# Branch products in pairs, lambda on ScalarE, bias turning in four pieces and value products with their low parts last, in a two-layer hybrid encoder

## The chip, the cores and the metric

The kernel runs on one core of one Trainium2 chip. The metric is device time in microseconds (us) of one execution. The engines are named as in the profile: PE is TensorE (matmuls and transposes), DVE is VectorE, ACT is ScalarE, POOL is GpSimd and SP is SyncE, which here issues the weight loads.

## The reference, cut to what matters

Two layers, each an FFN, a mixer and a second FFN, on 512 tokens of width 1024, all in fp32. The change touches the mixer alone:

```
qa, ka, va, qd, kd, vd, qc, kc, vc = jnp.split(h @ w_in[l], PROJ_OFFSETS, axis=-1)
ya = neighbourhood_attention(qa, ka, va, na_rpb[l])               # 8 heads, 2-D bias
# differential attention, 4 heads, two softmax maps each, T5 bias:
a = p[:, :, 0] - lam * p[:, :, 1]
yb = rms_norm(einsum(a, vd), subln_g) * (1.0 - lam_init)
yc = window_gqa(qc, kc, vc, gqa_sink[l], rel_bias_table)          # 8 query heads, 2 key heads
g = sigmoid(h @ w_gate[l] + b_gate[l])                            # 3 gates of width 1024
merged = g[0] * (ya @ w_branch[l, 0]) + g[1] * (yb @ w_branch[l, 1]) + g[2] * (yc @ w_branch[l, 2])
x = x + merged @ w_o[l]
```

## The kernel before

Activations stand turned, as 128 features by 512 tokens. Every fp32 operand of a product is split into a high and a low part, and a product is three matmuls for each 128 rows of the contraction: high weight by high input (L96), high weight by low input (L97) and, when all inputs have had these two, low weight by high input (L99). A weight tile is loaded by SP, its high part is cast on ACT (L82) and its low part is subtracted on DVE (L83). An input is split in the same way, by ACT L106 and DVE L108.

PSUM holds three buffers for products (`mm`), two for scores (`s`), two that transposes (`t`) and small statistics (`st`) share, and one for attention outputs and, once a layer, a fourth value block (`av`). A product takes a `mm` buffer, and gives it back when its reader is done: DVE L450 for a projection, DVE L797 for a gate, DVE L812 for a branch product.

The mixer writes its work down in an order made by hand. `beside(attention, steps, n)` takes eight attention steps, each with the transposes and value products left over from earlier steps, and puts some n of the listed projection, gate and merge steps between them. A scheduler then places the instructions of all of this on each engine, and may move them within it, so code that is written one product after another need not run so.

The places that the change and the prediction touch:

- `v_stacked` (L499 to L520) makes the values of the neighbourhood attention: four token blocks in four PSUM buffers (three `mm`, one `av`), all four filled in step over eight pieces of the contraction, then read by ACT L517 and DVE L518 in halves.
- `attend_diff` turns the head's bias on POOL (L675, one copy a head of 128x896), and after each pair of softmax maps takes the reciprocals of their sums on DVE (L739), multiplies the second by minus lambda on DVE (L740, 128x1), scales the second map on ACT (L741), and adds the two on DVE (L742). The result is transposed on PE (L681).
- `gqa_keys` projects keys and then values; the values, scaled by DVE L450, are transposed on PE (L832).
- `merge(i, mm)` makes two output tiles of branch i, each a product over the four 128-row pieces `yp` of that branch's attention output. The fourth piece comes last. For branch 1 it is made by DVE L714, then split by ACT L106 and DVE L108. The four merges of branch 2 stand at the end of the mixer, ahead of the output projection, with the attention's last fold ahead of them (ACT L568, DVE L569).

Of the kernel before, what the change touches and what calls it, by code (L numbers as in the profile page):

```python
# [13 lines left out]
AF = mybir.ActivationFunctionType  # L14
ALU = mybir.AluOpType

P = 128
# [16 lines left out]
def encoder(ctx: ExitStack, tc: tile.TileContext, a: dict, out: bass.AP):  # L34
# [51 lines left out]
    def mm_tile():  # L86
        return psum.tile([P, S], F32, tag="mm", name="mm", bufs=3)
# [4 lines left out]
    def product(ps, wparts, xhi, xlo):  # L92

        n = len(wparts)
        for k, (wh, wl) in enumerate(wparts):
            nc.tensor.matmul(ps, wh, xhi[k], start=k == 0, stop=False)  # L96
            nc.tensor.matmul(ps, wh, xlo[k], start=False, stop=False)  # L97
        for k, (wh, wl) in enumerate(wparts):
            nc.tensor.matmul(ps, wl, xhi[k], start=False, stop=k == n - 1)  # L99
# [74 lines left out]
    def reversed_view(t, last, dims):  # L174

        return bass.AP(tensor=t.tensor, offset=t.offset + last, ap=[list(t.ap[0]), *[[-s, n] for s, n in dims]])
# [252 lines left out]
    def mixer(l, h, nxt):  # L429
        with tc.tile_pool(name="mix", bufs=1) as mp:  # L430
# [68 lines left out]
            def v_stacked():  # L499

                ps = [mm_tile(), mm_tile(), mm_tile(), av_tile()]
                for c in range(4):
                    w = cols(weights(a["w_va"][l, c]), 2, S)
                    for k, (wh, wl) in enumerate(w, 2 * c):
                        for t in range(4):
                            ts = slice(t * P, (t + 1) * P)
                            nc.tensor.matmul(ps[t], h.hi[k][:, ts], wh, start=k == 0, stop=False)
                            nc.tensor.matmul(ps[t], h.lo[k][:, ts], wh, start=False, stop=False)
                            nc.tensor.matmul(ps[t], h.hi[k][:, ts], wl, start=False, stop=k == KC - 1)
                    yield  # L510
                v_na.extend(([], []))
                for t in range(4):
                    r = h.rs[:, t : t + 1]
                    for half in range(2):
                        v = mp.tile([P, 4, P], F32R, tag="v", name="vn", bufs=8)
                        pv = ps[t][:, half * 256 : half * 256 + 256].rearrange("p (h d) -> p h d", d=64)
                        nc.scalar.activation(v[:, :, 0:64], pv, AF.Copy, scale=r)  # L517
                        nc.vector.scalar_tensor_tensor(  # L518
                            out=v[:, :, 64:P], in0=pv, scalar=r, in1=f(v[:, :, 0:64]), op0=ALU.mult, op1=ALU.subtract
                        )  # L520
                        v_na[half].append(v)
                yield
# [145 lines left out]
            def attend_diff(head):  # L668
# [3 lines left out]
                db = work.tile([P, 640], F32, tag="acc", name="db", bufs=1)  # L672
                nc.sync.dma_start(db[:, 0:560], at(d_diff, head * 1024, [[1, 16], [64, 8], [1, 560]]))
                bias = mp.tile([P, 112, ROWS], F32, tag="pb", name="dpb", bufs=2)
                nc.gpsimd.tensor_copy(out=bias, in_=reversed_view(db, 559, [[1, 112], [GRID, ROWS]]))  # L675
                held = []

                def turn(half, jj, p, ph, pl):
# [38 lines left out]
                for half in range(2):  # L717
                    ph = mp.tile([P, 4, 2, P], F32R, tag="pt", name="ph", bufs=4)
                    pl = mp.tile([P, 4, 2, P], F32R, tag="pt", name="pl", bufs=4)
                    for jj in range(2):  # L720
                        j = 2 * half + jj
                        negm = small.tile([P, 4], F32, tag="negm", name="negm")
                        tot = small.tile([P, 4], F32, tag="tot", name="tot")
                        pc = []
                        for c in range(2):
                            ps = s_tile()
                            scores(ps, q[c], k[c], slice(j * P, j * P + P), slice(0, S))
                            pc.append(l_tile())
                            softmax(
                                pc[c],  # L730
                                ps,
                                bias[:, 48 - 16 * j : 112 - 16 * j].rearrange("p c r -> p (c r)"),
                                BIG,
                                negm[:, c : c + 1],
                                tot[:, c : c + 1],
                            )
                            if c == 0:
                                yield None
                        nc.vector.reciprocal(tot[:, 0:2], tot[:, 0:2])  # L739
                        nc.vector.tensor_tensor(out=tot[:, 1:2], in0=tot[:, 1:2], in1=nlam, op=ALU.mult)  # L740
                        nc.scalar.activation(pc[1], pc[1], AF.Copy, scale=tot[:, 1:2])  # L741
                        nc.vector.scalar_tensor_tensor(  # L742
                            out=pc[0], in0=pc[0], scalar=tot[:, 0:1], in1=pc[1], op0=ALU.mult, op1=ALU.add
                        )
                        yield lambda half=half, jj=jj, p=pc[0], ph=ph, pl=pl: turn(half, jj, p, ph, pl)
# [57 lines left out]
            def merge(i, mm):  # L803
                yh, yl = [t[0] for t in ys[i]], [t[1] for t in ys[i]]
                w = cols(weights(a["w_branch"][l, i, mm]), 8)
                for odd in range(2):
                    m = 2 * mm + odd
                    ps = mm_tile()
                    product(ps, w[4 * odd : 4 * odd + 4], yh, yl)
                    t = gates.pop((i, m))  # L810
                    o = merged[m] if i == 0 else t
                    nc.vector.scalar_tensor_tensor(out=o, in0=t, scalar=1.0, in1=ps, op0=ALU.add, op1=ALU.mult)  # L812
                    if i > 0:
                        nc.vector.tensor_tensor(out=merged[m], in0=merged[m], in1=t, op=ALU.add)
                    if i == 2:
                        mh[m] = mp.tile([P, S], F32R, tag="qk", name="mh", bufs=12)
                        nc.scalar.copy(mh[m], merged[m])
                        ml[m] = mp.tile([P, S], F32R, tag="v", name="ml", bufs=8)
                        nc.vector.tensor_tensor(out=ml[m], in0=merged[m], in1=f(mh[m]), op=ALU.subtract)
                yield  # L820

            def gqa_keys():
# [4 lines left out]
                    kd.append((t, swapped(t)))  # L827
                yield
                vf = project(21, 1.0, True)
                vt = t_tile()  # L830
                for t in range(4):
                    nc.tensor.transpose(vt[:, t, :], vf[:, t * P : (t + 1) * P], ident)  # L832
# [60 lines left out]
            beside(attend_diff(0), [qk(5), (None,), (None,), merge(0, 0), *g0(3, 4), merge(0, 1)], 8)  # L893
            beside(attend_diff(1), [g0(5)[0], merge(0, 2), qk(6), v_diff(1)], 6)
            beside(attend_diff(2), [*g0(6, 7), qk(7)], 4)
            beside(attend_diff(3), [merge(0, 3), gqa_keys(), gqa_queries(0), *g1(0, 1)], 6)
            beside(attend_gqa(0), [*g1(2), *[gqa_queries(p) for p in (1, 2, 3)], merge(1, 0), *g1(3)], 6)
            beside(attend_gqa(1), [*g1(4), merge(1, 1), *g1(5, 6), merge(1, 2), *g1(7)], 6)
            beside(attend_gqa(2), [merge(1, 3), *[gate(2, m, "v", 8) for m in range(3)]], 4)
            beside(attend_gqa(3), [gate(2, 3, "v", 8), *[gate(2, m) for m in (4, 5)]], 3)  # L900
# [114 lines left out]
```

## Time and profile before

| what | value |
|---|---|
| median of 3 runs (lowest to highest) | 2483.62 us (2482.66 to 2483.65) |
| the profiled execution's own time | 2485.75 us |
| its span in the trace | 2484.0 us |
| PE busy | 2465.3 us, 99% of the span, 11604 matmuls and transposes |
| DVE busy | 1294.3 us, 52% |
| ACT busy | 1053.8 us, 42% |
| POOL busy | 193.1 us, 8% |
| the chain that ended last | PE 97%, DVE 1%, ACT 1% |
| granted TensorE clock, mean | 0.999 of full speed |

Busy times are those of the trace. A matmul of 512 columns is listed with some 0.39 us, but the next one starts some 0.23 us after it, since they are pipelined. So a gap between the starts of two matmuls that is longer than that is time lost, also where the trace lists no idle time.

### The profile page before, as it was taken

How to read it: one execution, taken by the hardware profiler on the slowest of the kernel's cores; microseconds unless marked ns; L12 is line 12 of the kernel's file. 1: busy time of each engine (PE TensorE's matmuls, PEld its weight loads, DVE VectorE, ACT ScalarE, POOL GpSimd, SP SyncE). 2: the span in 40 equal slices, each digit the busy share in tenths (PEclk: the TensorE clock that was granted, in tenths of full speed). 3: DMA queues.
4: the chain of work that ended last, by engine and by line, in shares of the span. 5: the costliest groups of instructions: out<-in, count | busy, mean ns of one | idle time of the engine just before them, and what ended most of it. 6: DMA issues, size and time to landing. Idle time of an engine off the chain costs nothing.

```text
span 2484.0 us, 30196 instructions
## 1 busy us (share of the span) xinstructions
PE 2465.3 (99%) x11604; PEld 2054.7 (83%) x11604; DVE 1294.3 (52%) x2178; ACT 1053.8 (42%) x1776; POOL 193.1 (8%) x300
## 2 busy tenths in 40 slices
PE   8999999999999999999999999999999999999998
PEld 7888888888888888888888888888888888888887
DVE  5444335766666644443344443367676766444432
ACT  5333225755557433332232332267555664333322
POOL 2000003311000000000000000033110001000000
PEclk9999999999999999999999999999999999999999
DMA  5323344432322342233432324443322224332232
GB/s 169 102 94 100 119 131 127 118 103 78 93 85 86 124 128 97 95 98 119 133 107 94 101 91 131 140 118 107 98 86 92 86 83 148 119 115 93 95 100 68
DMA packets 80655, 265.24 MB, mean 107 GB/s; under 512 B 10904, under 2 KB 16328, under 8 KB 80512
## 3 DMA queue, kind: packets, MB, share of 16 engines
q1 hardware_dynamic: 67680, 226.59, 29.4%
q0 software_dynamic: 11680, 34.86, 4.9%
q8 instruction: 92, 1.51, 0.2%
q10 hardware_dynamic: 1152, 1.86, 0.2%
q14 instruction: 51, 0.42, 0.1%
HBM read 241.22 MB, written 12.62 MB: 102 GB/s over the span
## 4 chain that ended last, share of the span: by engine, by line
PE 97%; DVE 1%; ACT 1%; issue 0%; DMA 0%; SPq 0%; POOLq 0%; POOL 0%; ACTq 0%; DVEq 0%
PE mm L96 22%; PE mm L97 22%; PE mm L99 22%; PE mm L288 5%; PE mm L290 5%; PE mm L287 5%; PE av L597 2%; PE t L587 1%; PE s L542 1%; PE s L543 1%; PE av L698 1%; PE mm L492 1%; PE mm L491 1%; PE mm L389 1%; PE mm L387 1%; PE mm L388 1%
## 5 line engine op out<-in xcount | busy, mean ns | idle before, releaser
L96 PE MATMUL mm<-h,whi 128*128 128x512 f32 x2112 | 831.7, 394 | 0.2
L97 PE MATMUL mm<-l,whi 128*128 128x512 f32 x2112 | 825.0, 391 | 0.0
L82 ACT CAST whi<-raw 128x1024 fp32r<-128x1024 f32 (+1 forms) x414 | 429.9, 1039 | 715.3 <-PE mm L97 372.7
L83 DVE TENSOR_TENSOR wlo<-raw,whi 128x1024 fp32r<-128x1024 f32 (+1 forms) x414 | 500.6, 1209 | 294.3 <-ACT whi L82 179.7
L99 PE MATMUL mm<-h,wlo 128*128 128x512 f32 x2112 | 521.8, 390 | 0.0
L99 PEld LDWEIGHTS mm<-h,wlo 128*128 128x128 f32 x2112 | 396.7, 188 | 82.2
L96 PEld LDWEIGHTS mm<-h,whi 128*128 128x128 f32 x2112 | 397.0, 188 | 80.7 <-issue 0.8
L97 PEld LDWEIGHTS mm<-l,whi 128*128 128x128 f32 x2112 | 397.3, 188 | 79.4
L298 DVE TENSOR_TENSOR un<-mm,rb 128x512 f32<-128x512 f32 x87 | 60.1, 691 | 296.8 <-PE mm L99 296.8
L288 PE MATMUL mm<-g,whi 128*128 128x512 f32 x528 | 205.7, 390 | 0.0
L287 PE MATMUL mm<-g,whi 128*128 128x512 f32 x528 | 205.6, 389 | 0.0
L106 ACT CAST g<-un 128x512 fp32r<-128x512 f32 x88 | 54.5, 620 | 251.4 <-DVE un L299 251.4
L290 PE MATMUL mm<-g,wlo 128*128 128x512 f32 x528 | 131.4, 390 | 0.0
L295 DVE TENSOR_TENSOR gn<-mm,rb 128x512 f32<-128x512 f32 x88 | 60.8, 691 | 133.4 <-PE mm L99 133.4
L556 ACT ACTIVATE lg<-lg,negm 128x256 f32<-128x256 f32 (+1 forms) x192 | 114.0, 594 | 25.2 <-DVE negm L553 23.7
L61 POOL DMA_DIRECT2D d_x<-x x40 | 22.1, 553 | 1262.9 <-DVE x L246 1262.6
L288 PEld LDWEIGHTS mm<-g,whi 128*128 128x128 f32 x528 | 99.2, 188 | 20.5
L290 PEld LDWEIGHTS mm<-g,wlo 128*128 128x128 f32 x528 | 99.2, 188 | 20.5
L287 PEld LDWEIGHTS mm<-g,whi 128*128 128x128 f32 x528 | 99.1, 188 | 20.5
L296 ACT ACTIVATE gn<-gn 128x512 f32<-128x512 f32 x88 | 55.8, 634 | 123.6 <-DVE gn L295 123.6
L108 DVE TENSOR_TENSOR g<-un,g 128x512 fp32r<-128x512 f32 x88 | 60.9, 692 | 62.8 <-ACT g L106 62.8
L246 DVE SCALAR_TENSOR_TENSOR x<-mm,x 128x512 f32<-128x512 f32 x40 | 27.7, 692 | 109.1 <-PE mm L290 72.4
(223 smaller groups left out, 3037.8 us busy)
## 6 DMA issues: line engine op xcount, KB each, us to landing
raw<-in_w_gu SPq DMA_DIRECT2D x172, 512.0 KB, 3.4
raw<-in_w_down SPq DMA_DIRECT2D x48, 512.0 KB, 3.5
raw<-in_w_gate SPq DMA_DIRECT2D x48, 512.0 KB, 3.5
raw<-in_w_qk SPq DMA_DIRECT2D x44, 512.0 KB, 3.6
raw<-in_w_branch SPq DMA_DIRECT2D x24, 512.0 KB, 3.5
raw<-in_w_last SPq DMA_DIRECT2D x22, 512.0 KB, 3.5
d_x<-x POOLq DMA_DIRECT2D x40, 256.0 KB, 2.4
x<-d_x POOLq DMA_DIRECT2D x40, 256.0 KB, 2.9
```

Source lines behind the costliest of these rows:

```text
L82: nc.scalar.copy(hi[:, w], raw[:, w])
L83: nc.vector.tensor_tensor(out=lo[:, w], in0=raw[:, w], in1=f(hi[:, w]), op=ALU.subtract)
L96: nc.tensor.matmul(ps, wh, xhi[k], start=k == 0, stop=False)
L97: nc.tensor.matmul(ps, wh, xlo[k], start=False, stop=False)
L99: nc.tensor.matmul(ps, wl, xhi[k], start=False, stop=k == n - 1)
L108: nc.vector.tensor_tensor(out=lo, in0=src, in1=f(hi), op=ALU.subtract)
L287: nc.tensor.matmul(ps, w[k][0], ghi[c + k], start=c + k == 0, stop=False)
L288: nc.tensor.matmul(ps, w[k][0], glo[c + k], start=False, stop=False)
L290: nc.tensor.matmul(ps, w[k][1], ghi[c + k], start=False, stop=c + k == MF - 1)
L295: nc.vector.tensor_tensor(out=gn, in0=pg, in1=h.rb, op=ALU.mult)
L298: nc.vector.tensor_tensor(out=un, in0=pu, in1=h.rb, op=ALU.mult)
L556: nc.scalar.activation(p, p, AF.Exp, bias=negm, scale=-1.0, accum_out=total)
```

## The change

Five edits, all in the mixer, which runs once in each of the two layers.

1. `v_stacked`: for the first three weight tiles the high matmuls of both contraction pieces run first and the low ones behind them. With the last weight tile the four token blocks are finished one by one, each with its reads by ACT and DVE right behind.
2. The bias of a differential head is turned in four copies of 128x224 in place of one of 128x896.
3. The multiplication by minus lambda (128x1) is a ScalarE activation in place of a VectorE operation.
4. `merge`: the two output tiles are made side by side. Input by input, both take their two high matmuls; the low matmuls of the first and then of the second tile end it.
5. `gqa_keys` has one more `yield`, between the projection of the values and their transposes; the step counts of two `beside` calls go from 6 to 7 and from 6 to 5.

```
@@ -499,17 +499,30 @@
             def v_stacked():
 
                 ps = [mm_tile(), mm_tile(), mm_tile(), av_tile()]
-                for c in range(4):
+                def high(t, k, wh):
+                    ts = slice(t * P, (t + 1) * P)
+                    nc.tensor.matmul(ps[t], h.hi[k][:, ts], wh, start=k == 0, stop=False)
+                    nc.tensor.matmul(ps[t], h.lo[k][:, ts], wh, start=False, stop=False)
+
+                def low(t, k, wl):
+                    nc.tensor.matmul(ps[t], h.hi[k][:, t * P : (t + 1) * P], wl, start=False, stop=k == KC - 1)
+
+                for c in range(3):
                     w = cols(weights(a["w_va"][l, c]), 2, S)
-                    for k, (wh, wl) in enumerate(w, 2 * c):
+                    for k, (wh, _) in enumerate(w, 2 * c):
                         for t in range(4):
-                            ts = slice(t * P, (t + 1) * P)
-                            nc.tensor.matmul(ps[t], h.hi[k][:, ts], wh, start=k == 0, stop=False)
-                            nc.tensor.matmul(ps[t], h.lo[k][:, ts], wh, start=False, stop=False)
-                            nc.tensor.matmul(ps[t], h.hi[k][:, ts], wl, start=False, stop=k == KC - 1)
+                            high(t, k, wh)
+                    for k, (_, wl) in enumerate(w, 2 * c):
+                        for t in range(4):
+                            low(t, k, wl)
                     yield
+                w = cols(weights(a["w_va"][l, 3]), 2, S)
                 v_na.extend(([], []))
                 for t in range(4):
+                    for k, (wh, _) in enumerate(w, 6):
+                        high(t, k, wh)
+                    for k, (_, wl) in enumerate(w, 6):
+                        low(t, k, wl)
                     r = h.rs[:, t : t + 1]
                     for half in range(2):
                         v = mp.tile([P, 4, P], F32R, tag="v", name="vn", bufs=8)
@@ -672,7 +685,8 @@
                 db = work.tile([P, 640], F32, tag="acc", name="db", bufs=1)
                 nc.sync.dma_start(db[:, 0:560], at(d_diff, head * 1024, [[1, 16], [64, 8], [1, 560]]))
                 bias = mp.tile([P, 112, ROWS], F32, tag="pb", name="dpb", bufs=2)
-                nc.gpsimd.tensor_copy(out=bias, in_=reversed_view(db, 559, [[1, 112], [GRID, ROWS]]))
+                for c in range(0, 112, 28):
+                    nc.gpsimd.tensor_copy(out=bias[:, c : c + 28], in_=reversed_view(db, 559 - c, [[1, 28], [GRID, ROWS]]))
                 held = []
 
                 def turn(half, jj, p, ph, pl):
@@ -737,7 +751,7 @@
                             if c == 0:
                                 yield None
                         nc.vector.reciprocal(tot[:, 0:2], tot[:, 0:2])
-                        nc.vector.tensor_tensor(out=tot[:, 1:2], in0=tot[:, 1:2], in1=nlam, op=ALU.mult)
+                        nc.scalar.activation(tot[:, 1:2], tot[:, 1:2], AF.Copy, scale=nlam)
                         nc.scalar.activation(pc[1], pc[1], AF.Copy, scale=tot[:, 1:2])
                         nc.vector.scalar_tensor_tensor(
                             out=pc[0], in0=pc[0], scalar=tot[:, 0:1], in1=pc[1], op0=ALU.mult, op1=ALU.add
@@ -803,10 +817,15 @@
             def merge(i, mm):
                 yh, yl = [t[0] for t in ys[i]], [t[1] for t in ys[i]]
                 w = cols(weights(a["w_branch"][l, i, mm]), 8)
-                for odd in range(2):
+                both = [mm_tile(), mm_tile()]
+                for k in range(4):
+                    for ps, (wh, _) in zip(both, (w[k], w[4 + k])):
+                        nc.tensor.matmul(ps, wh, yh[k], start=k == 0, stop=False)
+                        nc.tensor.matmul(ps, wh, yl[k], start=False, stop=False)
+                for odd, ps in enumerate(both):
                     m = 2 * mm + odd
-                    ps = mm_tile()
-                    product(ps, w[4 * odd : 4 * odd + 4], yh, yl)
+                    for k in range(4):
+                        nc.tensor.matmul(ps, w[4 * odd + k][1], yh[k], start=False, stop=k == 3)
                     t = gates.pop((i, m))
                     o = merged[m] if i == 0 else t
                     nc.vector.scalar_tensor_tensor(out=o, in0=t, scalar=1.0, in1=ps, op0=ALU.add, op1=ALU.mult)
@@ -827,6 +846,7 @@
                     kd.append((t, swapped(t)))
                 yield
                 vf = project(21, 1.0, True)
+                yield
                 vt = t_tile()
                 for t in range(4):
                     nc.tensor.transpose(vt[:, t, :], vf[:, t * P : (t + 1) * P], ident)
@@ -893,8 +913,8 @@
             beside(attend_diff(0), [qk(5), (None,), (None,), merge(0, 0), *g0(3, 4), merge(0, 1)], 8)
             beside(attend_diff(1), [g0(5)[0], merge(0, 2), qk(6), v_diff(1)], 6)
             beside(attend_diff(2), [*g0(6, 7), qk(7)], 4)
-            beside(attend_diff(3), [merge(0, 3), gqa_keys(), gqa_queries(0), *g1(0, 1)], 6)
-            beside(attend_gqa(0), [*g1(2), *[gqa_queries(p) for p in (1, 2, 3)], merge(1, 0), *g1(3)], 6)
+            beside(attend_diff(3), [merge(0, 3), gqa_keys(), gqa_queries(0), *g1(0, 1)], 7)
+            beside(attend_gqa(0), [*g1(2), *[gqa_queries(p) for p in (1, 2, 3)], merge(1, 0), *g1(3)], 5)
             beside(attend_gqa(1), [*g1(4), merge(1, 1), *g1(5, 6), merge(1, 2), *g1(7)], 6)
             beside(attend_gqa(2), [merge(1, 3), *[gate(2, m, "v", 8) for m in range(3)]], 4)
             beside(attend_gqa(3), [gate(2, 3, "v", 8), *[gate(2, m) for m in (4, 5)]], 3)
```

The scheduler's order of instructions shows three of these places. In its rows the numbers behind the names are those of tiles, which differ between the two kernels, and x3 and x4 count instructions that stand in a row.

On DVE and ACT, first layer, at the fourth and last pair of maps of the second differential head. Before, on DVE: the maximum and biased scores of the second map (the two ISA rows), a weight split, the reciprocals, lambda's multiplication, the sum of both maps (L742), and a gate.

```order
L553 ISA lg_4878,negm_4860<-s_4875,dpb_4490 128x512
L553 ISA negm_4860 128x1
L83 TENSOR_TENSOR wlo_5132<-raw_5130,whi_5131 128x1024
L739 RECIPROCAL tot_4861<-tot_4861 128x2
L740 TENSOR_TENSOR tot_4861<-tot_4861,nlam_616 128x1
L742 SCALAR_TENSOR_TENSOR lg_4865<-lg_4865,tot_4861,lg_4878 128x512
L797 TENSOR_TENSOR z_4916<-mm_4891,rb_2728 128x512
```

After, on DVE:

```order
L566 ISA lg_4884,negm_4866<-s_4881,dpb_4493 128x512
L566 ISA negm_4866 128x1
L83 TENSOR_TENSOR wlo_5141<-raw_5139,whi_5140 128x1024
L753 RECIPROCAL tot_4867<-tot_4867 128x2
L756 SCALAR_TENSOR_TENSOR lg_4871<-lg_4871,tot_4867,lg_4884 128x512
L811 TENSOR_TENSOR z_4922<-mm_4897,rb_2728 128x512
```

After, on ACT: the two exponentials, lambda, the scaling of the second map, a weight cast, a gate.

```order
L569 ACTIVATE lg_4871,tot_4867<-lg_4871,negm_4866 128x512
L569 ACTIVATE lg_4884,tot_4867<-lg_4884,negm_4866 128x512
L754 ACTIVATE tot_4867<-tot_4867,nlam_616 128x1
L755 ACTIVATE lg_4884<-lg_4884,tot_4867 128x512
L82 CAST whi_5204<-raw_5203 128x1024
L813 ACTIVATE gate_4924<-z_4922,bg_280 128x512
```

The multiplication left DVE, where L753 and L756 are now neighbours, and stands on ACT between the exponentials and the scaling.

On PE, first layer, the fourth differential head with the values of the grouped attention. Before: the end of the value projection (`mm` with `wlo`), the scores of two maps, the transposes of the scaled values (L832), a statistics matmul, the next projection.

```order
L99 MATMUL mm_5326<-h6_2536,wlo_5322 128x512
L99 MATMUL mm_5326<-h7_2633,wlo_5322 128x512
L542 MATMUL s_5372<-qk_5163,qk_5068 128x512
L543 MATMUL s_5372<-qk_5163,qks_5074 128x512
L542 MATMUL s_5393<-qk_5166,qk_5071 128x512
L543 MATMUL s_5393<-qk_5166,qks_5077 128x512
L832 MATMUL t_5353<-ident_77,qn_5351 128x128 x4
L156 MATMUL st_5379<-ones_78,sqd_5318 128x1 x4
L96 MATMUL mm_5409<-h0_1955,whi_5404 128x512
```

After (L852 is the same transpose):

```order
L99 MATMUL mm_5338<-h6_2536,wlo_5334 128x512
L99 MATMUL mm_5338<-h7_2633,wlo_5334 128x512
L555 MATMUL s_5367<-qk_5172,qk_5077 128x512
L556 MATMUL s_5367<-qk_5172,qks_5083 128x512
L156 MATMUL st_5374<-ones_78,sqd_5330 128x1 x4
L695 MATMUL t_5381<-ident_77,lg_5251 128x128 x4
L555 MATMUL s_5405<-qk_5175,qk_5080 128x512
L556 MATMUL s_5405<-qk_5175,qks_5086 128x512
L96 MATMUL mm_5421<-h0_1955,whi_5416 128x512
L852 MATMUL t_5388<-ident_77,qn_5363 128x128 x4
```

Between the projection's end and the value transposes there stood four score matmuls. Now the statistics, the transposes of a head's map and the first matmul of the next projection stand there too.

On PE, first layer, `merge(1, 0)`: its first matmuls, with the transposes of the grouped attention around them. The first rows' `yp` tiles are the high (L96) and low (L97) parts of the first three inputs; the last row of before is the first matmul that needs the fourth input.

```order
L587 MATMUL t_5853<-ident_77,lg_5689 128x128 x3
L96 MATMUL mm_5865<-yp_4702,whi_5860 128x512
L97 MATMUL mm_5865<-yp_4704,whi_5860 128x512
L96 MATMUL mm_5865<-yp_5096,whi_5860 128x512
L97 MATMUL mm_5865<-yp_5098,whi_5860 128x512
L96 MATMUL mm_5865<-yp_5458,whi_5860 128x512
L97 MATMUL mm_5865<-yp_5460,whi_5860 128x512
L96 MATMUL mm_5880<-yp_4702,whi_5860 128x512
L97 MATMUL mm_5880<-yp_4704,whi_5860 128x512
L96 MATMUL mm_5880<-yp_5096,whi_5860 128x512
L97 MATMUL mm_5880<-yp_5098,whi_5860 128x512
L96 MATMUL mm_5865<-yp_5849,whi_5860 128x512
```

After (L823 and L824 are the new high matmuls; the fourth input comes behind the rows shown):

```order
L600 MATMUL t_5865<-ident_77,lg_5701 128x128 x3
L555 MATMUL s_5871<-qk_5294,qk_5451 128x384
L556 MATMUL s_5871<-qks_5297,qk_5451 128x384
L823 MATMUL mm_5894<-yp_4708,whi_5889 128x512
L824 MATMUL mm_5894<-yp_4710,whi_5889 128x512
L823 MATMUL mm_5895<-yp_4708,whi_5889 128x512
L600 MATMUL t_5882<-ident_77,lg_5728 128x128 x3
L824 MATMUL mm_5895<-yp_4710,whi_5889 128x512
L823 MATMUL mm_5894<-yp_5105,whi_5889 128x512
L824 MATMUL mm_5894<-yp_5107,whi_5889 128x512
L823 MATMUL mm_5895<-yp_5105,whi_5889 128x512
L824 MATMUL mm_5895<-yp_5107,whi_5889 128x512
```

Already before, the scheduler had put ten matmuls, four of them of the second tile, ahead of the first one with the fourth input. Now twelve stand ahead of it, with a score pair and three transposes among them; these transposes (`t_5882`) go to the buffer in which the statistics tile (`st_5855`) stood, which DVE reads in L728, the L714 of before.

## Rows read from the trace of the kernel before

**Rows 1.** The page: the span, and each engine's busy time, share and instructions.

```profile
span 2484.0 us, 30196 instructions
...
PE 2465.3 (99%) x11604; PEld 2054.7 (83%) x11604; DVE 1294.3 (52%) x2178; ACT 1053.8 (42%) x1776; POOL 193.1 (8%) x300
```

**Rows 2.** PE's waits: engine, line waited for, us in total, times, longest.

```profile
PE mm L343 <- ACT whi L324: 7.8, 2, 4.9
PE mm L96 <- ACT yp L106: 1.5, 4, 0.5
PE t L681 <- DVE lg L742: 0.6, 2, 0.3
PE t L832 <- DVE qn L450: 0.5, 2, 0.3
```

**Rows 3.** Timeline behind `v_stacked` (start, duration, engine, operation, [idle before]): PE, then DVE.

```profile
408.22 0.28 PE L542 MATMUL s<-qk 128*128 128x256 f32 x1
408.61 0.47 PE L96 MATMUL mm<-h,whi 128*128 128x512 f32 x1
408.91 0.40 PE L97 MATMUL mm<-l,whi 128*128 128x512 f32 x1
...
407.97 0.88 DVE L518 SCALAR_TENSOR_TENSOR vn<-mm,rs,vn 128x256 fp32r<-128x256 f32 x2 [0.54 <-ACT vn L517]
```

**Rows 4.** Timeline at the second head's last map: POOL, DVE, PE.

```profile
593.16 2.67 POOL L675 COPY dpb<-db 128x896 f32<-128x896 f32 x1 [19.48 <-issue]
...
594.28 1.56 DVE L740 TENSOR_TENSOR tot<-tot,nlam 128x1 f32<-128x1 f32 x1
596.70 0.75 DVE L742 SCALAR_TENSOR_TENSOR lg<-lg,tot 128x512 f32<-128x512 f32 x1 [0.85 <-ACT lg L741]
...
596.89 0.39 PE L543 MATMUL s<-qk,qks 128*128 128x512 f32 x1
597.60 0.63 PE L681 MATMUL t<-ident,lg 128*128 128x128 f32 x4 [0.32 <-DVE lg L742]
```

**Rows 5.** All instructions of lines 740 and 785: ns min/median/max, first and last start.

```profile
L740 DVE TENSOR_TENSOR tot<-tot,nlam x32: 150/159/1572, 522.0 to 1900.3; 128x1 f32<-128x1 f32 x32
...
L785 ACT ACTIVATE se<-negm,sink x64: 277/282/291, 675.3 to 2033.3; 128x1 f32<-128x1 f32 x64
```

**Rows 6.** Timeline at the value transposes of `gqa_keys`: PE, then DVE.

```profile
643.74 0.39 PE L543 MATMUL s<-qk,qks 128*128 128x512 f32 x1
644.38 0.66 PE L832 MATMUL t<-ident,qn 128*128 128x128 f32 x4 [0.25 <-DVE qn L450]
...
643.26 1.07 DVE L450 SCALAR_TENSOR_TENSOR qn<-mm,rb 128x512 f32<-128x512 f32 x1 [1.74 <-PE mm L99]
```

**Rows 7.** Timeline at `merge(1, 0)`: PE, ACT, DVE.

```profile
696.50 0.39 PE L97 MATMUL mm<-yp,whi 128*128 128x512 f32 x1
697.37 0.73 PE L96 MATMUL mm<-yp,whi 128*128 128x512 f32 x2 [0.48 <-ACT yp L106]
...
696.72 0.60 ACT L106 CAST yp<-o 128x512 fp32r<-128x512 f32 x1
...
694.92 0.74 DVE L714 SCALAR_TENSOR_TENSOR o<-o,sg,st 128x512 f32<-128x512 f32 x1
...
698.41 0.67 DVE L108 TENSOR_TENSOR yp<-o,yp 128x512 fp32r<-128x512 f32 x1
```

**Rows 8.** Timeline of PE at `merge(2, 0)`: ten matmuls up to 818.59, then the wait.

```profile
816.52 0.39 PE L96 MATMUL mm<-yp,whi 128*128 128x512 f32 x1
...
818.59 0.39 PE L97 MATMUL mm<-yp,whi 128*128 128x512 f32 x1
819.23 0.96 PE L96 MATMUL mm<-yp,whi 128*128 128x512 f32 x3 [0.25 <-ACT yp L106]
```

**Rows 9.** Timeline of DVE behind the last branch product of the layer.

```profile
838.65 0.69 DVE L812 SCALAR_TENSOR_TENSOR gate<-gate,mm 128x512 f32<-128x512 f32 x1 [0.43 <-PE mm L99]
839.25 1.22 DVE L83 TENSOR_TENSOR wlo<-raw,whi 128x1024 fp32r<-128x1024 f32 x1
```

## The prediction

> **What bounds the kernel now.** I read the page first. PE is busy 2465.3 of 2484.0 us [rows 1], and none of the five edits removes a matmul, so all that can be won is time in which PE stands still. The reader is to see that this is 18.7 us as listed, over the whole kernel. The second view is PE's list of waits [rows 2]: 7.8 us of it lie at the start of the kernel, where nothing is changed. The other three entries are all in the mixer, and each comes in twos or fours, so once or twice a layer: the fourth input of a branch product, the sum of two differential maps, and the values of the grouped attention. The third view is the timeline at each of these places, and behind `v_stacked`, whose wait is too short for that list. There I take start-to-start distances. Ten matmuls of 512 columns from 816.52 to 818.59 are (818.59 − 816.52)/9 = 0.23 us apart [rows 8]; what a distance has above this is lost. A matmul of 256 columns takes half of it, 0.12 (an estimate by columns).
>
> **The change part by part, for one layer.**
>
> *Value blocks one by one.* Behind `v_stacked` the scores' matmul starts at 408.22 and the next product at 408.61: 0.39 − 0.12 = 0.27 lost, and 0.30 − 0.23 = 0.07 at the matmul after it [rows 3]. The product needs a PSUM buffer that DVE L518 reads up to 407.97 + 0.88 = 408.85, all four blocks being ready at about the same time. After the change the first block is complete 18 matmuls (4.1 us) ahead of the last one, and its ACT and DVE reads run beside these; the first product takes its buffer. The cover of 4.1 us is some ten times the 0.34 lost, so I take the whole **0.34**. If the cover were gone, it would be nothing gained. The low parts that come last in each weight tile change the order of matmuls alone. The wait at the start of this stage, for a buffer that a projection holds, has seven matmuls of the two free buffers ahead of it before and after; it stays.
>
> *Lambda and the bias.* At the second head's last pair of maps DVE L740, a 128x1 multiplication, takes 1.56 us and ends at 595.84; the POOL copy of the next head's bias ends at 593.16 + 2.67 = 595.83 [rows 4]. The same line's median is 0.159 us [rows 5]. So the copy holds it, and the sum L742, which starts 0.86 after L740's end, runs 596.70 to 597.45. PE is done with the scores at 596.89 + 0.23 = 597.12 and starts to transpose at 597.60: 0.71 − 0.23 = **0.48** lost [rows 4]. With lambda on ACT nothing of DVE stands between: 594.28 + 0.28 (a 128x1 activation, L785 [rows 5]) + 0.86 = 595.42 for L742's start, 596.17 for its end, 0.95 ahead of PE. If L742, with two inputs in SBUF, is itself held to the copy's end, it ends at 595.83 + 0.75 = 596.58, still 0.54 ahead. The Trainium skill (SBUF — State Buffer, "SBUF: two separate sides") says that DVE, where it has two SBUF inputs, and a GpSimd operation that reads SBUF exclude each other for the whole instruction; by it, four copies bound any one hold to a quarter, 0.67 (an estimate from the copy's row), which matters only if the copies come later than now. The price is lambda itself: 0.28 in place of 0.16 in 16 pairs of maps a layer, 0.12 each. Mostly L742 is ready ahead of PE, or PE waits for something else; I charge **0.1** a layer, between nothing and 16 × 0.12 = 1.9. POOL is busy 8% [rows 1]; its 24 more copies of a quarter each replace eight, and cost PE nothing.
>
> The Trainium skill (ScalarE: Activation LUTs, "Rules for kernel authors") speaks against this edit: multiplications belong on VectorE. The two medians above, 0.282 on ACT and 0.159 on DVE, agree with it for one instruction; what it would make of the time is the third rival.
>
> *The extra yield.* The value transposes wait for DVE L450, which runs from 643.26 to 644.33: 643.74 to 644.38 is 0.64, so **0.41** lost [rows 6]. Now a statistics matmul, four transposes and one matmul of 512 columns come between as well: 0.23 + 4 × 0.06 (a quarter of 0.23 each, by columns) = 0.47 at least, above the 0.41. So the wait goes. New is that these transposes take the buffer in which the statistics stand, until DVE has read them behind L450. The read is short, but I have no row for it here: between nothing and the whole 0.41 given back; I take nothing, since three PE groups lie between. The other steps that the counts 7 and 5 move (`merge(1, 0)` by one attention step) go past no load that PE waits for.
>
> *Branch products in pairs.* This has two places. At `merge(1, 0)` PE waits for the high part of the fourth input: 696.50 to 697.37 is 0.87, 0.64 lost, and the two matmuls from 697.37 last 0.73 in place of 0.23 + 0.39, so 0.11 more: 0.75 [rows 7]. The diff suggests that six more matmuls now come ahead, but the order shows that ten of them stood there already; they are twelve now, with a pair of 384-column scores (2 × 0.17) and three transposes ahead too. Working back from 696.50, the first branch matmul was at 696.50 − 9 × 0.23 = 694.43; it is now at 694.77, and the fourth PE slot, the three transposes, at 695.46. They need the buffer that DVE L714 leaves at 694.92 + 0.74 = 695.66: 0.20 lost, and 0.1 of restart as above. The fourth input is then wanted at 695.76 + 3 × 0.06 + 9 × 0.23 = 698.0, and its high part is there at 696.72 + 0.60 = 697.32. Its low part is wanted 0.23 later, at 698.2. Before, DVE L108 made it from 698.41 to 699.08, behind a weight split of 1.22. That split is now behind L108, a 384-column softmax pass is ahead of it (0.55 as an estimate, three quarters of L714's 0.74): 698.41 − 1.22 + 0.55 + 0.67 = 698.4, so 0.2 lost, and a restart of 0.1. Of 0.75 some 0.6 come back at the two new waits: I take **0.1** won, between −0.1 and 0.75. At `merge(2, 0)` it is 818.59 to 819.23, 0.64 − 0.23 = 0.41, and (0.96 − 0.85) = 0.11 behind it [rows 8]. Here ten of the branch's matmuls, without the two that the scheduler put ahead of the last attention product, already ran ahead of the wait: the order has twelve before and twelve after. The chain ahead of the fourth input is untouched. I take **nothing**, between nothing and 0.52.
>
> *Sum.* 0.34 + 0.48 + 0.41 + 0.1 − 0.1 = 1.23 a layer, 2.5 for two, since the list counts the same waits in both [rows 2]. The profiled execution took 2485.75 us with a span of 2484.0; it would be 2483.3 with 2481.5. The median of the runs is 2.1 below the profiled one, so 2483.62 − 2.5 = **2481.1 us**.
>
> **The rivals.**
>
> 1. *All these waits go*: 0.34 + 0.48 + 0.41 + 0.75 + 0.52 = 2.50 a layer, 5.0 in all, 2478.6 us. For it: the pairing in code leaves both places with their twelve matmuls ahead. Against it: the scheduler had put ten or twelve there without it [rows 8].
> 2. *The waits move and PE gets nothing*: each one ends one step later at another late reader, as at `merge(1, 0)`, 2483.5 us. For it: DVE makes almost all releases and is busy 52% on average [rows 1], far more at these places. Against: at the first three places the cover found is longer than the wait.
> 3. *Lambda's longer hop reaches PE in every pair*: 32 × 0.12 = 3.8 us on the forecast, 2484.9 us. Against: before the change, L742 is late in PE's list only twice [rows 2].
> 4. *Slower by PSUM buffers*: a merge now takes two of the three `mm` buffers at once, and the next merge's second tile reuses the first one's buffer only six matmuls, 6 × 0.23 = 1.38 us, after its last matmul. That matmul's 0.39 and L812's 0.69 [rows 9] fit in with 0.30 to spare. If a weight split of 1.22 stands ahead of L812, PE waits 1.22 − 0.30 + 0.11 = 1.03 at each of the three joints of the last four merges: 6.2 us over two layers, 2487.3 us. It eats the gain from 0.30 + 2.5/6 = 0.72 of lateness on. Against: DVE stood idle 0.43 until the product's end, with the split behind L812 and not ahead of it [rows 9]; other merges have gates between them.
>
> **How the numbers follow.** A measurement of this kernel can tell some 0.2% from no change, 5.0 us: below 2478.6 is faster, above 2488.6 slower. Chances: the forecast (1 to 4 us won) 0.65, all waits gone 0.13, nothing won 0.12, lambda's hop 0.05, buffers 0.05. Half of the second case and a little of the first lies below 2478.6: faster 0.10. Slower needs the fourth rival at more places than three a layer: 0.03. Same 0.87. The range takes in the first two rivals' times and the spread of the runs shown (some 0.5 us about their median), 2478.0 to 2483.9, and leaves out the last two and little else.
>
> **What the profile after would show.** L740's successor (128x1 on ACT) at some 0.28 us 32 times, and no wait of the map transposes for the sum; no wait of the value transposes for L450's result; behind `v_stacked` a distance of 0.23 where it was 0.39; the wait for the fourth input gone at `merge(1, 0)` with two small ones in its place, for the statistics' reader and for the input's low part; at `merge(2, 0)` the same 0.4 as before. It is wrong if the waits for the fourth input go at both places (first rival), if PE's waits name DVE as the last reader of `mm` buffers at the last merges (fourth), or if a stage that I priced at nothing, the moved `merge(1, 0)` above all, has grown.

## The result, and the profile after

The changed kernel takes 2489.19 us (median of 22 runs, 2481.73 to 2494.29), the kernel before 2483.55 (22 runs, 2482.4 to 2484.83): ratio 1.0021, interval 1.0015 to 1.0027. In this comparison it is slower by 0.2%, and its runs spread over 12.6 us where those of before lie within 2.4. The forecast was 2481.1 us. The profiled execution took 2485.53 us with a span of 2483.7, so it is one of the quicker ones (fifth of 22) and shows less of the loss than the median has. Of the experiments below, one execution of before_store_on_act (8665 us, mean granted clock 0.403) and one of act_store_counts (2722 us, 0.85) were far slower than the rest; no trace shows them, they are not explained, and the ratios leave them out.

PE's waits after (columns as in [rows 2]):

```profile
PE mm L343 <- ACT whi L324: 5.2, 2, 5.0
PE mm L96 <- ACT h L125: 1.6, 1, 1.6
PE mm L97 <- DVE l L127: 0.9, 2, 0.5
PE st L156 <- ACT sqd L718: 0.8, 2, 0.4
PE mm L823 <- ACT yp L106: 0.5, 2, 0.3
PE t L600 <- DVE o L728: 0.4, 2, 0.2
PE mm L504 <- DVE qn L450: 0.2, 1, 0.2
```

The waits for the sum of two maps and for the values of the grouped attention are gone from [rows 2]; of the four for a fourth input two are left. New are the second, third, fourth and sixth line. The last line, at the start of `v_stacked`, is no mark of the change: the profile of before_store_on_act, which has none of its edits, has the same wait with 0.5. The first line is at the start of the kernel, where nothing was changed; that start differs from execution to execution, and here it is 3.5 us shorter than in the profile of before (PE comes to its first statistics matmul at 25.84 and not at 29.30). The timeline of PE at the places that answer to [rows 3], [rows 4] and [rows 6]:

```profile
404.33 0.62 PE L508 MATMUL av<-wlo,h 128*128 128x512 f32 x2
404.78 0.39 PE L96 MATMUL mm<-h,whi 128*128 128x512 f32 x1
...
593.07 0.39 PE L556 MATMUL s<-qk,qks 128*128 128x512 f32 x1
593.30 0.60 PE L695 MATMUL t<-ident,lg 128*128 128x128 f32 x4
...
641.02 0.40 PE L96 MATMUL mm<-h,whi 128*128 128x512 f32 x1
641.26 0.60 PE L852 MATMUL t<-ident,qn 128*128 128x128 f32 x4
```

At each of the three a 512-column matmul is followed after 0.23 or 0.24: nothing is lost. So the three large terms came as forecast. Then the new wait, and the places that answer to [rows 7] and [rows 8]:

```profile
677.97 0.39 PE L97 MATMUL mm<-l,whi 128*128 128x512 f32 x1
678.75 1.05 PE L156 MATMUL st<-ones,sqd 128*128 128x1 f32 x8 [0.39 <-ACT sqd L718]
...
691.13 0.39 PE L823 MATMUL mm<-yp,whi 128*128 128x512 f32 x1
691.70 0.52 PE L600 MATMUL t<-ident,lg 128*128 128x128 f32 x3 [0.18 <-DVE o L728]
...
814.26 0.39 PE L824 MATMUL mm<-yp,whi 128*128 128x512 f32 x1
814.89 0.96 PE L823 MATMUL mm<-yp,whi 128*128 128x512 f32 x3 [0.25 <-ACT yp L106]
```

The statistics of the fourth differential head lose 0.78 − 0.23 = 0.55. The transposes in `merge(1, 0)` lose 0.34, at the place that was named and in place of 0.64; `merge(2, 0)` loses 0.40 as before. Compared at equal work of PE (the starts of the same matmul by its number in PE's order), the first mixer is 0.9 us shorter than before and the second 0.7. What ate this, and more, stands behind the mixer, in the first product of the second FFN, where the kernel before lost nothing:

```profile
880.85 0.39 PE L97 MATMUL mm<-l,whi 128*128 128x512 f32 x1
882.84 0.50 PE L96 MATMUL mm<-h,whi 128*128 128x512 f32 x1 [1.61 <-ACT h L125]
883.88 0.79 PE L97 MATMUL mm<-l,whi 128*128 128x512 f32 x1 [0.54 <-DVE l L127]
884.47 3.15 PE L99 MATMUL mm<-h,wlo 128*128 128x512 f32 x8
```

1.99 − 0.23 = 1.76, 1.04 − 0.23 = 0.81 and 0.59 − 0.23 = 0.36 are lost to the last normalised tile `h`, and the eight matmuls behind it take 3.15, where eight take 7 × 0.23 + 0.39 = 2.0 else. Together 4.1 us. The second layer loses 0.7 more at the same place. So the span of this profile is nearly that of before by luck: 3.5 shorter at the start, 1.6 shorter in the mixers, 4.8 longer here. The granted clock (the third number from the right) in two windows there:

```profile
883.00:885.00 2.00, 1.46 (x4) 0.96 (x5) 1.43 (x3) 0.60 (x2) 0.65 (x2) 0.63 0.43 117
885.00:888.00 3.00, 3.00 (x14) 2.46 (x12) 0.28 (x1) 0.75 (x1) 0.00 (x0) 0.68 0.78 272
```

After PE had stood idle for 1.61 us, a part of these windows ran at the lower level, 1.2 GHz; before, both windows show 1.00.

Why `h` is late is seen on POOL's queue, which stores the residual `x` (L61), whose new value DVE L246 makes from each output projection, and loads the old value of the tile after next into one of two buffers (L56). Before:

```profile
846.47 0.61 POOL L61 DMA_DIRECT2D d_x<-x  x1 [157.31 <-DVE x L246]
849.57 0.55 POOL L56 DMA_DIRECT2D x<-d_x  x1 [2.49 <-ACT whi L82]
850.98 0.55 POOL L61 DMA_DIRECT2D d_x<-x  x1 [0.85 <-DVE x L246]
854.08 0.55 POOL L56 DMA_DIRECT2D x<-d_x  x1 [2.56 <-DMA d_x<-x]
```

After, with DVE's L246:

```profile
843.28 0.61 POOL L61 DMA_DIRECT2D d_x<-x  x1 [162.12 <-DVE x L246]
846.42 0.55 POOL L56 DMA_DIRECT2D x<-d_x  x1 [2.53 <-DVE x L246]
847.11 0.55 POOL L61 DMA_DIRECT2D d_x<-x  x1
853.07 0.55 POOL L56 DMA_DIRECT2D x<-d_x  x1 [5.41 <-ACT sq L136]
853.71 0.56 POOL L61 DMA_DIRECT2D d_x<-x  x1
...
842.29 0.69 DVE L246 SCALAR_TENSOR_TENSOR x<-mm,x 128x512 f32<-128x512 f32 x1 [2.51 <-PE mm L99]
845.46 0.69 DVE L246 SCALAR_TENSOR_TENSOR x<-mm,x 128x512 f32<-128x512 f32 x1 [0.69 <-PE mm L99]
...
857.83 0.69 DVE L246 SCALAR_TENSOR_TENSOR x<-mm,x 128x512 f32<-128x512 f32 x1 [3.84 <-DMA x<-d_x]
```

Before, the first two stores are 4.51 us apart, POOL waits for DVE ahead of each, and the load behind it starts 3.1 after it, when the store has landed and its buffer is free. After, the first two projections end 845.46 − 842.29 = 3.17 apart. The second store is ready at 846.15, but stands in the queue behind the load, which waits for the first store to land (the profile names L246, but that had ended 0.27 earlier; the load is 3.14 behind the first store, as before). It is issued right behind the load, 0.96 after it is ready, and the next load comes 5.96 after it, not 3.1: most of the delay is the longer time to landing, not the wait in the queue. From here on each store stands right behind a load: the cycle is some 6 us where PE makes a tile every 24 × 0.227 = 5.4, and from 857.83 on L246 waits for its load: it starts 3.2 to 4.8 behind the load's issue, also where the profile names another releaser. The transfers' own view of the output projection (the last number is the median from issue to landing in us): before,

```profile
d_x<-x POOLq DMA_DIRECT2D x8, 256.0 KB, 2.5
```

and after:

```profile
d_x<-x POOLq DMA_DIRECT2D x8, 256.0 KB, 4.8
```

### The profile page after: what moved, and what is told of

It reads as the page before. It is cut to its first block, busy times and chain, and to the rows that moved or that the text cites. A ratio compares the mean times of both kernels' runs of the same rounds, so it can differ in the third digit from the quotient of the medians.

```text
span 2483.7 us, 30227 instructions
## 1 busy us (share of the span) xinstructions
PE 2466.1 (99%) x11604; PEld 2053.5 (83%) x11604; DVE 1285.7 (52%) x2146; ACT 1063.1 (43%) x1808; POOL 198.1 (8%) x324
## 4 chain that ended last, share of the span: by engine, by line
PE 97%; DVE 1%; ACT 1%; issue 1%; DMA 0%; SPq 0%; POOLq 0%; POOL 0%; DVEq 0%; ACTq 0%
PE mm L99 20%; PE mm L97 20%; PE mm L96 20%; PE mm L287 5%; PE mm L290 5%; PE mm L288 5%; PE av L610 2%; PE mm L828 2%; PE mm L824 2%; PE mm L823 2%; PE t L600 1%; PE s L555 1%; PE s L556 1%; PE av L712 1%; PE mm L494 1%
## 5 line engine op out<-in xcount | busy, mean ns | idle before, releaser
L96 PE MATMUL mm<-h,whi 128*128 128x512 f32 x2112 | 830.5, 393 | 1.6 <-ACT h L125 1.6
L97 PE MATMUL mm<-l,whi 128*128 128x512 f32 x2112 | 824.5, 390 | 0.9 <-DVE l L127 0.9
L96 PEld LDWEIGHTS mm<-h,whi 128*128 128x128 f32 x2112 | 396.7, 188 | 82.3 <-ACT h L125 2.0
L97 PEld LDWEIGHTS mm<-l,whi 128*128 128x128 f32 x2112 | 397.0, 188 | 81.1 <-DVE l L127 1.7
L61 POOL DMA_DIRECT2D d_x<-x x40 | 22.2, 554 | 1251.7 <-DVE x L246 1251.1
L246 DVE SCALAR_TENSOR_TENSOR x<-mm,x 128x512 f32<-128x512 f32 x40 | 27.7, 692 | 111.8 <-PE mm L290 72.8
```

## The experiments

Theory A is this queue. The rivals: B, that lambda, the bias or moved transfers made the time spread; C, that pairs wait for PSUM buffers (the fourth rival of the prediction). Times are medians of 11 runs, with the kernel before on the same chip beside them and the ratio's interval.

**tail_single**

```diff
-                both = [mm_tile(), mm_tile()]
+                if i < 2:
+                    both = [mm_tile(), mm_tile()]
...
+                    else:
+                        ps = mm_tile()
+                        product(ps, w[4 * odd : 4 * odd + 4], yh, yl)
```

> The changed kernel, with the four merges of branch 2 (the tail of the mixer) written as before, one product after the other; everything else of the change stays. Theory A (the pairing in the tail lets the first two output projections end 3.2 us apart in place of 4.3, and the residual's stores and loads on POOL's one queue then stand right behind one another and fall behind the projections): the two ends are 4.3 us apart again, the wait for the last normalised tile at the start of the second FFN (1.8 us and more in the first layer of the changed kernel's profile) is gone, 2482 us (2483.6 less the 0.9 and 0.75 that the two mixers gained in that profile), and its executions lie within 3 us of each other. Theory B (other transfers that the change moved, or lambda and the bias, make the time spread): 2488 to 2489 us, spread over some 10 us as the changed kernel. Theory C (the pairs wait for PSUM buffers in all merges): half of the loss stays, some 2486 us.

Measured: 2482.21 (2481.45 to 2484.1) with 2483.16 before, 0.9996 (0.9987 to 1.0004). POOL's queue at the same place:

```profile
843.17 0.61 POOL L61 DMA_DIRECT2D d_x<-x  x1 [161.03 <-DVE x L246]
846.31 0.55 POOL L56 DMA_DIRECT2D x<-d_x  x1 [2.52 <-ACT whi L82]
847.68 0.54 POOL L61 DMA_DIRECT2D d_x<-x  x1 [0.82 <-DVE x L246]
850.79 0.55 POOL L56 DMA_DIRECT2D x<-d_x  x1 [2.57 <-DMA d_x<-x]
```

The stores are 4.51 apart again, the load follows 3.1 behind, and PE has no wait for `h`. As A expects; B and C fall for the large loss. (Later in this layer one load comes 5.36 behind its store here too, 858.47 to 863.83, and in the kernel before one 4.67, 861.77 to 866.44; in both the queue makes it up and PE loses nothing.) The changed kernel itself was not timed beside this run and the next three, on this chip.

**tail_pair_only** (the other way round: before, with `if i == 2:` around the pairs)

> The kernel before, with only the four merges of branch 2 made in pairs. Theory A: the output projections' first two ends are 3.2 us apart, stores stand right behind loads on POOL's queue from the second tile on, and the time is 2485 to 2494 us with a spread of several us and a median near 2489 to 2490. Theory B: 2483.6 us within 1.2, as before. Theory C: 2485 to 2486 us with waits of PE for VectorE's branch-product reads in the tail.

Measured: 2485.29 (2483.37 to 2489.64), 1.0009 (1.0001 to 1.0018). The sign and the spread are A's, the size is short of it. In its profile the second store stands behind the load too (848.58, with the next load at 853.09), but the queue recovers later in this layer; in the second layer PE loses some 0.4 for the last tile.

**outputs_close** (before, with the first two output projections side by side)

```diff
+            for k in range(KC):
+                for ps, w in zip(both, first):
+                    nc.tensor.matmul(ps, w[k][0], mh[k], start=k == 0, stop=False)
+                    nc.tensor.matmul(ps, w[k][0], ml[k], start=False, stop=False)
```

> The kernel before, with no edit of the change, but the first two output projections made side by side, so that they end 8 matmuls (1.8 us) apart. Theory A: closeness of these two ends is the trigger, whatever makes it, so the time is above 2485 us and spreads as the changed kernel's does; the loads of the third tile and on land after the product that they are added to. Theories B and C: nothing of the change is in it, 2483.6 us within 1.2, perhaps 0.2 less each layer since the wait for the last merged tile is covered.

Measured: 2485.37 (2483.52 to 2487.74), 1.0008 (0.9999 to 1.0017). The median and the spread are those of the pairs in the tail, with no edit of the change, but the interval just reaches no change: that two outputs close together are enough is pointed to and not shown. The pattern is not quite the same either: the second store is issued ahead of the first load (848.43 and 849.25), and stores stand right behind loads only from the fourth on; PE then loses 0.7 at the head of the second FFN in the first layer.

**store_on_act**

```diff
-        nc.gpsimd.dma_start(residual[m], t)
+        nc.scalar.dma_start(residual[m], t)
```

> The changed kernel, with the residual's stores issued on ScalarE's queue, which reads the same tile next anyway, and the loads left on POOL's. Theory A: a store waits no longer for a load ahead of it on the queue, the load of the tile after next is issued as soon as its buffer's store has landed, no projection waits for its residual; 2482 us and a spread under 3 us with both pairs kept. Theory B: 2488 to 2489 us. If the transfers themselves have become slow and not the queue, the median stays above 2485.

Measured: 2481.69 (2481.05 to 2483.86), 0.9995 (0.9986 to 1.0004). The stores land in a median of 2.0:

```profile
d_x<-x ACTq DMA_DIRECT2D x8, 256.0 KB, 2.0
```

All five edits are in it, the two ends are 3.17 apart as in the changed kernel, and the loss is gone. So it is the stores' place in POOL's queue that costs, not the closeness alone, nor the pairs. The edit changes two things, though: a store stands behind no load any more, and the ACT queue lands a store sooner by itself (a median of 2.0 against 2.5 in the two profiles without the change). This run does not tell them apart.

**changed_again, no_lambda_bias, no_value_blocks, no_yield_counts** (the changed kernel itself, and with one of the other edits undone)

```diff
-                        nc.scalar.activation(tot[:, 1:2], tot[:, 1:2], AF.Copy, scale=nlam)
+                        nc.vector.tensor_tensor(out=tot[:, 1:2], in0=tot[:, 1:2], in1=nlam, op=ALU.mult)
...
-            beside(attend_diff(3), [merge(0, 3), gqa_keys(), gqa_queries(0), *g1(0, 1)], 7)
+            beside(attend_diff(3), [merge(0, 3), gqa_keys(), gqa_queries(0), *g1(0, 1)], 6)
```

> The changed kernel itself, for the comparison on one chip with the three runs beside it. Theory A: 2485 to 2494 us with a median of 2487 to 2490, and residual stores right behind loads on POOL's queue in both layers. If its median is near the 2485.3 of the pairs in the tail alone, the other edits add nothing to the loss.

> The changed kernel with lambda on VectorE and the bias turned in one copy, as before. The wait of the map transposes for the sum, 0.48 to 0.5 us a layer, comes back, and some 0.1 is given back. Theory A: the tail is untouched, so the median stays with the changed kernel, 2487 to 2490 us. Theory B (lambda or the bias' four copies on POOL's queue make the spread): 2483 us and a spread under 3 us.

> The changed kernel with the value products of the neighbourhood attention as before. The 0.38 us a layer behind that stage come back. Theory A: the median stays at 2487 to 2490 us. Theory B' (the low parts last hold the weight buffers longer and shift the weight loads): below 2485.

> The changed kernel without the extra yield and with both step counts at 6 again. The wait of the value transposes for their scaled values (0.43 us a layer) comes back, and the wait of a statistics matmul for ScalarE's squares at 678.75 in the changed kernel's profile (0.65 us a layer, which the kernel before did not have) goes, so each mixer is some 0.2 us faster. Theory A: the median stays at 2487 to 2490 us, the tail being untouched.

Measured, with 2483.55 before: 2484.53 (2481.98 to 2488.36), 2486.12 (2483.91 to 2491.76), 2488.34 (2483.19 to 2491.74) and 2484.04 (2481.82 to 2485.18). The ratios are 1.0005 (0.9996 to 1.0014), 1.0015 (1.0006 to 1.0024), 1.0016 (1.0007 to 1.0025) and 1.0001 (0.9992 to 1.0009), so two of the four can't be told from the kernel before. Of the medians A had only no_value_blocks right: the changed kernel itself was 1.0 above before on this chip, and 5.6 in the first comparison. no_yield_counts, whose tail is untouched, has the smallest loss and spread of the four; whether the moved steps have a part in the loss is not shown. What the four profiles agree on is the place. At equal work, and up to some 0.2 at the start of `v_stacked` that differs between executions, each mixer differs from the changed kernel's only by the edit undone: 0.38 more behind the value products, 0.5 more at the sum, 0.5 more at the value transposes but 0.7 less at the statistics. All else is lost at the head of the second FFN or right behind it, and by very different amounts, 0 to 8.1 us in a layer. The longest wait in the changed kernel run again, in its second layer:

```profile
2115.07 0.50 PE L96 MATMUL mm<-h,whi 128*128 128x512 f32 x1 [2.70 <-ACT h L125]
```

The clock is the other half of the size. Where the longest idle time of PE at this head was 0.9 or less, the granted clock stayed at 2.4 GHz in every profile, and a layer lost 2.0 at most. Behind the idles of 1.61 (the changed kernel's first profile), 2.70 (the row above) and 2.97 (no_value_blocks, second layer) it fell to 1.2 GHz, and the layers lost 4.1, 5.2 and 8.1. Of the 8.1 the two waits make 3.9; the rest went in slower instructions of PE, matmuls 0.43 apart in place of 0.23, in a stretch with a granted clock of 0.50 of full speed:

```profile
2115.82 0.79 PE L96 MATMUL mm<-h,whi 128*128 128x512 f32 x1 [2.97 <-ACT h L125]
...
2123.00 0.63 PE L97 MATMUL mm<-l,whi 128*128 128x512 f32 x1
2123.43 0.63 PE L96 MATMUL mm<-h,whi 128*128 128x512 f32 x1
...
2120.00:2125.00 5.00, 5.00 (x17) 4.30 (x16) 1.39 (x2) 0.00 (x0) 1.57 (x2) 0.50 0.44 125
```

**before_store_on_act** (the kernel before, with the edit of store_on_act)

> The kernel before, with only the residual's stores issued on ScalarE's queue. Theory A: in the kernel before no projection waits for its residual, so there is nothing to win: 2483.5 us, between 2483.0 and 2484.0. If the queue itself had cost something before, it would be below 2482.5, and the 2481.7 of the changed kernel with these stores would not be the gain of its five edits.

Measured: 2483.54, with 2483.16 before (0.9999, 0.999 to 1.0009): nothing shows that the queue cost something before, as A expects.

**act_store_counts** (store_on_act, with the second count at 6)

```diff
-            beside(attend_gqa(0), [*g1(2), *[gqa_queries(p) for p in (1, 2, 3)], merge(1, 0), *g1(3)], 5)
+            beside(attend_gqa(0), [*g1(2), *[gqa_queries(p) for p in (1, 2, 3)], merge(1, 0), *g1(3)], 6)
```

> The changed kernel with the residual's stores on ScalarE's queue and the second step count at 6 again (the extra yield and the count 7 stay). The statistics matmul of the fourth head stands 24 matmuls of a projection behind the head's products again, and not 8, so its wait for the squares (0.65 us a layer) goes, and twelve matmuls stand ahead of the fourth input in merge(1, 0) with no transposes among them, which leaves 0.2 to 0.3 of its wait of 0.75. Theory A with this: 1.3 to 1.7 us under the 2481.7 of the stores alone, 2480.0 to 2480.4, with a spread under 3 us. If the moved statistics are not the cause of that wait, it stays at 2481.7.

Measured: 2481.20, with 2483.16 before: 0.9990 (0.9981 to 0.9999), the lowest median of all, 2 us under the kernel before. The wait for the squares is gone from PE's list, which supports its cause; against store_on_act, on another chip, the median fell by 0.5 and not by 1.3, though at equal work, from behind the start of `v_stacked`, the mixers of this run are 1.35 and 1.4 shorter than before, where those of store_on_act are 0.8 and 0.7 shorter.

## Why the prediction was wrong

*Value blocks, the sum of two maps, the extra yield*: right. The terms 0.34, 0.48 and 0.41 came as 0.38, 0.50 and 0.49 a layer at equal work. Lambda's price was right too, 0.1 a layer; its activations take more than the 0.28 that was taken from L785 [rows 5]:

```profile
L754 ACT ACTIVATE tot<-tot,nlam x32: 282/295/297, 517.9 to 1898.8; 128x1 f32<-128x1 f32 x32
```

*Branch products in pairs*: right at `merge(2, 0)`. At `merge(1, 0)` the two new waits came where they were put, 0.34 and, at the input's low part, 0.04 and 0.11 behind it, so 0.26 was won in the first layer (0.14 in the second), where 0.1 was taken.

*The moved steps* failed: "The other steps that the counts 7 and 5 move (`merge(1, 0)` by one attention step) go past no load that PE waits for." Loads were the wrong thing to look for alone. With the count 5 the statistics matmul of the fourth head stands 8 projection matmuls behind the head's value products, which the squares are made of, and not 24, and ACT's squares come 0.55 too late for it; with the matmul behind it, which starts some 0.1 late, 0.65 a layer. With the count at 6 it is gone (no_yield_counts, act_store_counts). This term, which the prediction put at nothing, is the main reason why the net of a mixer was 0.7 to 0.9 in place of 1.23.

*What decided* was outside the sum. The fourth rival put the danger of the pairs in the tail, but in PSUM buffers; no wait of PE for a branch product's reader shows. The step that failed is "*Branch products in pairs.* This has two places." There is a third: the last two merged tiles are now finished four matmuls apart, so the last one is ready later, 5.6 us behind the first matmul of the output projections where it was 4.6, and the scheduler fills this time with ten matmuls of the second output projection where five stood before (24 less 3.17/0.227 and less 4.31/0.227). That draws the ends of the first two projections from 4.3 to 3.2 us together, and what hangs on these ends, a store and a load of the residual in one queue, had 0.85 us of idle time ahead of the second store before. From there on loads come too late for the projections, the last normalised tile for PE, and 4.8 us went at the heads of the second FFNs in this profile, up to 9.8 in that of no_value_blocks. The prediction looked at the projection's inputs and not at what it sends out. tail_single and store_on_act, which take this away in two ways, give 2482.2 and 2481.7, where 2481.1 was forecast. That is 1.0 and 1.5 under the kernel before and not 2.5; the moved steps' 2 × 0.65 is about what lacks.

*Open*: why the same kernel lost 5.6 us in one comparison and 1.0 in another, and why tail_pair_only lost 2.1. The place is the same in all profiles that lose, and the clock's fall adds to the longer waits; but how long each store takes behind a load (5.96 once and 4.51 in another run) was not controlled, so how often and how far the queue falls behind is not explained. The 512 KB weight loads of the same stretch land later too (a median of 4.3 us in the changed kernel, 3.7 before); which slows which is not shown.

The Trainium skill (DMA: Bandwidth & Descriptors, "Rules for kernel authors") says that spreading transfers over issuing engines does not help bandwidth, since they share the same DMA engines, and saves only time to issue them. Here moving the stores to ACT's queue removed the loss with the same bytes: a store stands behind no load there, and the time to landing fell from 4.8 to 2.0. As to bandwidth no run here tells against the page.

## What to carry to other kernels

When an edit moves the end of a product, follow what leaves with that end, too: the reader, its store, and what stands in the store's queue. A queue in which a load waits for one store ahead of the next store has a cycle time; if that is near the time of a tile, a shift of one microsecond at the start is made up late (tail_pair_only, first layer) or not at all (the changed kernel's profile), and shows as spread over the runs and as a wait far behind. In this kernel it helped to put the store on the queue of an engine that waits for the same tile anyway.

## What was not expected of the hardware

The stores of 256 KB behind the first mixer, seven of the eight issued right behind a load of 256 KB on POOL's queue, landed after a median of 4.8 us (4.5 in the second layer), against 2.5 in the kernel before, where POOL had mostly stood idle ahead of them, and 2.0 from ACT's queue (2.4 in the second layer of store_on_act). The POOL copies in four pieces took 3.51 us in all at the place of [rows 4], where the one copy took 2.67.
